# Two transformer-like blocks on one core: FFN up products with a wide operand, two FFN steps on GpSimd, first loads in halves

## The chip, the cores and the metric

The kernel runs on one core of a Trainium2 chip. The time is the device time of one execution in microseconds (us); the profile is one execution recorded by the hardware profiler. The engines are named TensorE (PE in the rows; PEld is its weight load), VectorE (DVE), ScalarE (ACT), GpSimd (POOL) and SyncE (SP, which issues most of the DMAs).

## The reference

Two residual blocks follow each other on an input x of 256 positions by 1024 features, all in float32. The first has a state-space branch and an LRU branch, whose results are gated and merged, and then a gated FFN; the second has four branches (delta rule, spatial gating, window attention, memory attention). The part that the change rewrites is the FFN of the first block:

```python
h = rmsnorm(x, ffn_pre_norm[l])
up = causal_dwconv(h @ w_ffn_up[l], ffn_conv_w[l], ffn_conv_b[l])   # 1024 -> 6144, 3 taps
f_gate, f_val = jnp.split(up, 2, axis=-1)
f = (jax.nn.gelu(f_gate, approximate=True) * f_val) @ w_ffn_down[l]  # 3072 -> 1024
x = x + rmsnorm(f, ffn_post_norm[l])
```

## The kernel before

Every large product runs in a split form: an operand is cut into a high part (rounded by a copy to the 32-bit matmul format) and a low part (operand less high part), and hi x hi, hi x lo and lo x hi are added up in PSUM. The activation's two parts lie side by side in one tile HX, so that `hx[:, k]` is the high part's 256 positions followed by the low part's 256.

The weights come as one long list of chunks, each of two halves of 128 x 1024 (512 KB). The class `Weights` loads the halves in order on SyncE's queue (`load`, line 87) into three raw buffers, makes the high half on ScalarE (line 112) and the low half on VectorE (line 113), and holds five halves of each. `next` is called once a chunk and has the halves split up to five ahead of the chunk's first. `split_pieces` does the same for the first two halves in four pieces each, so that the first product can start early.

There are three ways to run a chunk. `proj_fm` (lines 434 to 455) takes 48 matmuls of 256 columns: `mm3` three times over eight k and two groups of 128 output features; its result lies in PSUM. With `kouter` it goes over k outside. `proj_wide` (lines 457 to 473) takes 32 matmuls: for every k and group, the low weights with the high part (256 columns), and the high weights with both parts at once (512 columns); the second half of the bank is then copied to SBUF by ScalarE (line 471) and added to the first by VectorE (line 472), so its result lies in SBUF. `proj_tm` is the form with positions on the partitions.

The FFN up projection is 12 pairs of chunks (lines 1075 to 1090): the gate chunk (a = 0) and the value chunk (a = 1) of 256 features each. Each goes through `proj_fm`, then a convolution of three taps (`conv`: the last tap with the bias on ScalarE, line 607, the other two on VectorE, line 610). Then come a GELU on ScalarE (line 1086), the product of the two on VectorE (line 1087), and the split of the product into FH (ScalarE, line 353) and FL (VectorE, line 354), the operands of the down projection. TensorE's instructions run in the order of the program; those of the other engines are put in order by a planner, except in the first part of the program, where ScalarE's and VectorE's are in the order written. PSUM has four banks for these products (`pp`), and temporaries come from two rotating sets (`t` with five buffers, `pt` with four).

At the start (lines 276 to 295) SyncE issues the transposed activations XT in two transfers of 512 KB, each followed by a weight half, then one more half, then x; the columns of parameters that the first scaling needs come over ScalarE's queue.

Of the kernel before, what the change touches and what calls it, by code (L numbers as in the profile page):

```python
# [8 lines left out]
F32 = mybir.dt.float32  # L9
F32R = mybir.dt.float32r  # L10
AF = mybir.ActivationFunctionType
ALU = mybir.AluOpType
# [6 lines left out]
HW = 1024  # L19
# [47 lines left out]
class Weights:  # L67
# [14 lines left out]
    def load(self, n):  # L82
        n = min(n, len(self.halves))
        while self.nd < n:
            j = self.nd
            raw = self.pool.tile([P, HW], F32, tag="wraw", name=f"wraw{j}", bufs=self.raw_bufs)
            self.loaded = self.nc.sync.dma_start(raw, self.halves[j])
            self.raw[j] = raw
            self.nd += 1

# [106 lines left out]
def two_blocks_kernel(  # L197
# [27 lines left out]
    nc = tc.nc  # L225
# [12 lines left out]
    def pbank(name):  # L238
        return pp.tile([P, 512], F32, tag="pp", name=name)

    def act8(tag, name, dt=F32, n=NT):
        return big.tile([P, n, S], dt, tag=tag, name=name)

    def hilo(name):

        t = big.tile([P, NT, 2, S], F32R, tag="HX", name=name)
        return t[:, :, 0, :], t[:, :, 1, :], t

    def tmp(name, n=512, tag="t", bufs=NTP):
        return tp.tile([P, n], F32, tag=tag, bufs=bufs, name=name)  # L250

    def v2(ap):
        return ap.rearrange("p (j t) -> p j t", j=2)
# [19 lines left out]
    W = Weights(tc, wp, chunks, 3, 5)  # L273
# [3 lines left out]
    pc = cp.tile([P, NCOL], F32, name="pc")  # L277
    nc.scalar.dma_start(pc[:, 0:8], pcol[:, 0:8])
    XT = act8("b2", "XT")
    for g in range(2):  # L280
        nc.sync.dma_start(XT[:, 4 * g : 4 * g + 4, :],
                          xT[g].rearrange("p (k t) -> p k t", k=4))
        W.load(g + 1)
    W.load(3)
    wsmall = cp.tile([P, 8, 24], F32, name="wsmall")
    pr = cp.tile([P, NROW], F32, name="pr")
# [65 lines left out]
    def split(hi, lo, src):  # L352
        i = nc.scalar.copy(hi, src)
        nc.vector.tensor_tensor(out=lo, in0=src, in1=hi.bitcast(F32), op=ALU.subtract)
        return i
# [72 lines left out]
    def mm3(o, wh, wl, xh, xl, first, last):  # L428

        nc.tensor.matmul(o, wh, xh, start=first, stop=False)  # L430
        nc.tensor.matmul(o, wh, xl, start=False, stop=False)  # L431
        nc.tensor.matmul(o, wl, xh, start=False, stop=last)  # L432

    def proj_fm(name, xh, xl, kouter=False):

        wh, wl = W.next()
        if kouter:
            ps = [pbank(f"{name}_{j}")[:, 0:S] for j in range(2)]
            for k in range(8):
                for j in range(2):  # L440
                    f = slice(j * P, (j + 1) * P)
                    mm3(ps[j], wh[k][:, f], wl[k][:, f], xh[:, k, :], xl[:, k, :],
                        k == 0, k == 7)
                if k % 2 == 1 and k < 7:
                    yield
            return ps, None
        b = pbank(name)
        ps = [b[:, 0:S], b[:, S : 2 * S]]
        for j in range(2):
            f = slice(j * P, (j + 1) * P)  # L450
            for k in range(8):
                mm3(ps[j], wh[k][:, f], wl[k][:, f], xh[:, k, :], xl[:, k, :], k == 0, k == 7)
                if k % 4 == 3 and j + k < 8:
                    yield
        return ps, v2(b)

    def proj_wide(name, hx, o=None):

        wh, wl = W.next()
        ps = [pbank(f"{name}_{j}") for j in range(2)]  # L460
        o = v2(tmp(f"{name}_s")) if o is None else o
        for j in range(2):
            f = slice(j * P, (j + 1) * P)
            for k in range(8):
                a = (ps[j][:, 0:S], wl[k][:, f], hx[:, k, 0, :])
                b = (ps[j], wh[k][:, f], hx[:, k].rearrange("p a t -> p (a t)"))
                for i, p in enumerate((b, a) if k == 0 else (a, b)):
                    nc.tensor.matmul(*p, start=k + i == 0, stop=k == 7 and i == 1)  # L468
                if k % 4 == 3 and j + k < 8:
                    yield  # L470
            nc.scalar.copy(o[:, j, :], ps[j][:, S : 2 * S])
            nc.vector.tensor_tensor(out=o[:, j, :], in0=ps[j][:, 0:S], in1=o[:, j, :], op=ALU.add)
        return [o[:, j, :] for j in range(2)]
# [126 lines left out]
    def conv(outs, ps, wname, tiles, n, taps, bname=None):  # L600

        for o, p, i in zip(outs, ps, tiles):
            w = col(wname, (taps - 1) * n + i)
            if bname is None:
                nc.scalar.activation(o, p, AF.Identity, scale=w)
            else:
                nc.scalar.activation(o, p, AF.Identity, scale=w, bias=col(bname, i))
        for o, p, i in zip(outs, ps, tiles):
            for d in range(1, taps):
                nc.vector.scalar_tensor_tensor(  # L610
                    o[:, d:S], in0=p[:, 0 : S - d], scalar=col(wname, (taps - 1 - d) * n + i),
                    in1=o[:, d:S], op0=ALU.mult, op1=ALU.add)


    HH, HL, HX = hilo("HX1")
# [353 lines left out]
    def block1(HH, HL, HX):  # L969

        late = []
        for p in range(4):
            ps, b = yield from proj_fm(f"ly{p}", HU, LU, p == 0)
            late.append((p, ps, b))
            while late and "rms" in wv.events:
                i, ps, b = late.pop(0)
                o = GY[:, 2 * i : 2 * i + 2, :]
                if b is not None:
                    nc.vector.tensor_tensor(
                        out=o, in0=b, in1=rbc.unsqueeze(1).to_broadcast([P, 2, S]), op=ALU.mult)  # L980
# [7 lines left out]
        for p in (4, 5, 0, 1, 2, 3):  # L988
            ps, _ = yield from proj_fm(f"xbc{p}", HH, HL)
# [15 lines left out]
        for p in range(4):  # L1005
            ps = yield from proj_wide(f"lx{p}", HX)
# [12 lines left out]
        for i in range(4):  # L1019
            n, c = divmod(i, 2)  # L1020
            q = slice(512 * c, 512 * c + 512)
# [15 lines left out]
        for c in range(2):  # L1037
            q = slice(512 * c, 512 * c + 512)
# [3 lines left out]
                    out=MG[:, tt, q], in0=ps, in1=G[0][:, tt, q], op=ALU.mult))  # L1042
# [4 lines left out]
        for c in range(2):  # L1047
            q = slice(512 * c, 512 * c + 512)
# [11 lines left out]
        HH, HL, HX = hilo("HX2")  # L1060
# [6 lines left out]
        for p in range(2):  # L1067
            _, b = yield from proj_fm(f"mk{p}", em["h"], em["l"])
# [4 lines left out]
        FH = [act8(f"b{(3, 6, 7)[i]}", f"FH{i}", F32R) for i in range(3)]  # L1073
        FL = [act8(f"b{(9, 1, 8)[i]}", f"FL{i}", F32R) for i in range(3)]
        for p in range(12):
            cv = []
            for a in range(2):
                ps, _ = yield from proj_fm(f"fu{a}_{p}", HH, HL, p + a == 0)
                c = v2(tmp(f"fc{a}_{p}"))
                i = 24 * a + 2 * p  # L1080
                conv([c[:, 0, :], c[:, 1, :]], ps, "ffn_conv_w", (i, i + 1), 48, 3,
                     "ffn_conv_b")
                cv.append(c)
                if a == 0:
                    yield
            nc.scalar.activation(cv[0], cv[0], AF.Gelu_apprx_tanh)
            nc.vector.tensor_tensor(out=cv[0], in0=cv[0], in1=cv[1], op=ALU.mult)
            q = slice(2 * (p % 4), 2 * (p % 4) + 2)
            last = split(FH[p // 4][:, q, :], FL[p // 4][:, q, :], cv[0])
            yield  # L1090

        O = []
        HH, HL, HX = hilo("HX3")
# [635 lines left out]
    def program():  # L1729
        with tc.manual_schedule(engines={nc.scalar.engine, nc.vector.engine}):  # L1730
            constants()
            for g in range(2):
                for k, _ in enumerate(W.split_pieces(4)):
                    feature(4 * g + k, XT, HU, LU)
                more_loads(g)
            W.split(4)
            for tt in range(2):
                nc.scalar.activation(NRM[:, 0:1024], X[:, tt, :], AF.Square,
                                     accum_out=rx[:, tt : tt + 1])
            nc.scalar.activation(rx, rx, AF.Sqrt, bias=eps1, scale=1.0 / D)  # L1740
            nc.vector.reciprocal(rx, rx)
            dtab.append(small_w(0, 16, "wdt"))
            baab.append(small_w(16, 8, "wba"))
            nc.scalar.activation(ea, row("ssm_a_log"), AF.Exp)
            nc.scalar.activation(ea2, row("a_log_2"), AF.Exp)
            nc.vector.tensor_scalar(nlam, pc[:, lamc : lamc + 8], -1.0, None, op0=ALU.mult)
        yield from block1(HH, HL, HX)
# [139 lines left out]
```

## Time and profile before

| | us |
|---|---|
| median of 3 runs (lowest to highest) | 826.16 (826.12 to 826.82) |
| the profiled execution | 825.72 |
| its span, first to last instruction | 824.0 |
| TensorE busy | 809.6 (98%) |
| VectorE busy | 612.2 (74%) |
| ScalarE busy | 524.6 (64%) |
| GpSimd busy | 61.0 (7%) |

Busy shares are means over stages that differ. A matmul's recorded duration overlaps with the next one's, so its price is the distance from one start to the next. A wait is put down to the release that came last. Transfers are shown by their issue; when they landed shows in who waited for them.

### The profile page before, as it was taken

The numbers are of one execution on the slowest core, as the hardware profiler recorded it, in microseconds if no ns is written. First come the engines' busy times: TensorE is split into PE (matmuls) and PEld (weight loads), VectorE is DVE, ScalarE is ACT, GpSimd is POOL, SyncE is SP. The second block draws the span as 40 slices with busy tenths as digits, with TensorE's granted clock in tenths as the row PEclk, the third lists the DMA queues.
The fourth block names the chain that finished last, engine by engine and source line by source line (L and its number), as shares of the span: only waits on it lengthen the run. The fifth ranks groups of instructions, "written<-read, shape, count | busy, mean of one in ns | idle before, by whom it ended". The sixth has DMA issues, their size and how long they took to land.

```text
span 824.0 us, 13302 instructions
## 1 busy us (share of the span) xinstructions
PE 809.6 (98%) x5060; PEld 721.0 (87%) x5060; DVE 612.2 (74%) x1026; ACT 524.6 (64%) x820; POOL 61.0 (7%) x101
## 2 busy tenths in 40 slices
PE   6999999999999999999999999999999999999997
PEld 6999888888889999999988889888888888888886
DVE  5989789889689788888744697877786647566583
ACT  7575988895656666565643478956976555544452
POOL 0000000000110000000000100028830000000000
PEclk9999999999999999999999999999999999999999
DMA  8545435556754655555555544542454344555551
GB/s 310 204 172 212 153 104 207 177 205 201 257 186 149 216 189 185 182 177 191 201 196 193 192 158 151 182 157 104 169 156 149 130 143 167 202 190 192 190 193 52
DMA packets 41248, 147.12 MB, mean 179 GB/s; under 512 B 4896, under 2 KB 5152, under 8 KB 41056
## 3 DMA queue, kind: packets, MB, share of 16 engines
q1 hardware_dynamic: 40464, 145.35, 51.1%
q0 software_dynamic: 576, 0.92, 0.5%
q8 instruction: 40, 0.66, 0.3%
q14 instruction: 24, 0.20, 0.1%
q10 hardware_dynamic: 144, 0.00, 0.0%
HBM read 144.94 MB, written 1.31 MB: 177 GB/s over the span
## 4 chain that ended last, share of the span: by engine, by line
PE 92%; DVE 5%; ACT 1%; DMA 1%; issue 1%; DVEq 0%; SPq 0%; ACTq 0%
PE z L468 8%; PE fu L432 6%; PE fu L431 6%; PE fu L430 6%; PE g L430 5%; PE g L432 5%; PE g L431 5%; PE lx L468 3%; PE fd L431 3%; PE fd L432 3%; PE fd L430 3%; PE up L430 2%; PE up L431 2%; PE up L432 2%; PE o L432 2%; PE o L430 2%
## 5 line engine op out<-in xcount | busy, mean ns | idle before, releaser
L113 DVE TENSOR_TENSOR wlo<-wraw,whi 128x1024 fp32r<-128x1024 f32 x256 | 311.9, 1226 | 131.6 <-ACT whi L112 130.1
L112 ACT CAST whi<-wraw 128x1024 fp32r<-128x1024 f32 x256 | 266.3, 1049 | 198.4 <-PE fu L431 48.0
L430 PE MATMUL fu<-HX,whi 128*128 128x256 f32 x384 | 108.7, 283 | 0.0
L431 PE MATMUL fu<-HX,whi 128*128 128x256 f32 x384 | 108.7, 283 | 0.0
L432 PE MATMUL fu<-HX,wlo 128*128 128x256 f32 x384 | 108.7, 283 | 0.0
L430 PE MATMUL g<-whi,HX 128*128 128x512 f32 x192 | 76.7, 399 | 0.0
L432 PE MATMUL g<-whi,HX 128*128 128x512 f32 x192 | 74.9, 390 | 0.0
L431 PE MATMUL g<-wlo,HX 128*128 128x512 f32 x192 | 74.8, 390 | 0.0
L430 PEld LDWEIGHTS fu<-HX,whi 128*128 128x128 f32 x384 | 73.7, 192 | 0.0
L431 PEld LDWEIGHTS fu<-HX,whi 128*128 128x128 f32 x384 | 73.7, 192 | 0.0
L432 PEld LDWEIGHTS fu<-HX,wlo 128*128 128x128 f32 x384 | 73.7, 192 | 0.0
L468 PE MATMUL z<-HX,whi 128*128 128x512 f32 x192 | 70.1, 402 | 0.0
L468 PE MATMUL z<-HX,wlo 128*128 128x256 f32 x192 | 51.0, 286 | 0.0
L610 DVE SCALAR_TENSOR_TENSOR fc<-fu,pc,fc 128x255 f32<-128x255 f32 (+1 forms) x96 | 43.8, 478 | 1.6
L432 PEld LDWEIGHTS g<-whi,HX 128*128 128x128 f32 x192 | 36.0, 188 | 7.7
L431 PEld LDWEIGHTS g<-wlo,HX 128*128 128x128 f32 x192 | 36.1, 188 | 7.2
L430 PEld LDWEIGHTS g<-whi,HX 128*128 128x128 f32 x192 | 36.1, 188 | 7.2
L431 PE MATMUL fd<-wlo,FH 128*128 128x512 f32 (+1 forms) x120 | 41.7, 347 | 0.0
L430 PE MATMUL fd<-whi,FH 128*128 128x512 f32 (+1 forms) x120 | 41.6, 347 | 0.0
L432 PE MATMUL fd<-whi,FL 128*128 128x512 f32 (+1 forms) x120 | 41.6, 347 | 0.0
L468 PEld LDWEIGHTS z<-HX,whi 128*128 128x128 f32 x192 | 35.5, 188 | 6.8 <-issue 0.9
L468 PEld LDWEIGHTS z<-HX,wlo 128*128 128x128 f32 x192 | 36.2, 189 | 1.5
(539 smaller groups left out, 1922.7 us busy)
## 6 DMA issues: line engine op xcount, KB each, us to landing
wraw<-in_w_in_dram SPq DMA_DIRECT2D x130, 512.0 KB, 3.8
wraw<-in_w_fu_dram SPq DMA_DIRECT2D x48, 512.0 KB, 3.8
wraw<-in_w_fd_dram SPq DMA_DIRECT2D x24, 512.0 KB, 3.7
wraw<-in_w_o_dram SPq DMA_DIRECT2D x16, 512.0 KB, 3.5
wraw<-in_w_up_dram SPq DMA_DIRECT2D x16, 512.0 KB, 3.4
wraw<-in_w_pa_dram SPq DMA_DIRECT2D x8, 512.0 KB, 3.6
wraw<-in_w_pb_dram SPq DMA_DIRECT2D x8, 512.0 KB, 4.4
wraw<-in_w_mk_dram SPq DMA_DIRECT2D x4, 512.0 KB, 4.1
```

What stands on the lines that cost most here:

```text
L112: nc.scalar.copy(hi, raw)
L113: nc.vector.tensor_tensor(out=lo, in0=raw, in1=hi.bitcast(F32), op=ALU.subtract)
L430: nc.tensor.matmul(o, wh, xh, start=first, stop=False)
L431: nc.tensor.matmul(o, wh, xl, start=False, stop=False)
L432: nc.tensor.matmul(o, wl, xh, start=False, stop=last)
L468: nc.tensor.matmul(*p, start=k + i == 0, stop=k == 7 and i == 1)
L610: nc.vector.scalar_tensor_tensor(o[:, d:S], in0=p[:, 0 : S - d], scalar=col(wname, (taps - 1 - d) * n + i), in1=o[:, d:S], op0=ALU.mult, o ...
```

## The change

Three things change. The first transfers: XT now comes in pieces of two, two and four k-tiles, and the first weight half in two halves, interleaved as XT piece, weight piece, XT piece, weight piece, XT piece (`between` is called behind each weight piece); then the second and third half come as before. The FFN up projection: all chunks but the first go through `proj_wide`, with the sum in a temporary of the `pt` set. The FFN's product and the low part of it run on GpSimd for the first eleven pairs, on VectorE for the last; the copy to FH stays on ScalarE.

```diff
--- before.py
+++ after.py
@@ -84,7 +84,12 @@
         while self.nd < n:
             j = self.nd
             raw = self.pool.tile([P, HW], F32, tag="wraw", name=f"wraw{j}", bufs=self.raw_bufs)
-            self.loaded = self.nc.sync.dma_start(raw, self.halves[j])
+            if j == 0:
+                for q in (slice(0, HW // 2), slice(HW // 2, HW)):
+                    self.nc.sync.dma_start(raw[:, q], self.halves[j][:, q])
+                    self.between()
+            else:
+                self.loaded = self.nc.sync.dma_start(raw, self.halves[j])
             self.raw[j] = raw
             self.nd += 1
 
@@ -277,10 +282,15 @@
     pc = cp.tile([P, NCOL], F32, name="pc")
     nc.scalar.dma_start(pc[:, 0:8], pcol[:, 0:8])
     XT = act8("b2", "XT")
-    for g in range(2):
-        nc.sync.dma_start(XT[:, 4 * g : 4 * g + 4, :],
-                          xT[g].rearrange("p (k t) -> p k t", k=4))
-        W.load(g + 1)
+    pieces = [(0, 2), (2, 4), (4, 8)]
+
+    def x_piece():
+        a, b = pieces.pop(0)
+        v = xT[a // 4].rearrange("p (k t) -> p k t", k=4)
+        nc.sync.dma_start(XT[:, a:b, :], v[:, a % 4 : a % 4 + b - a, :])
+
+    x_piece()
+    W.between = x_piece
     W.load(3)
     wsmall = cp.tile([P, 8, 24], F32, name="wsmall")
     pr = cp.tile([P, NROW], F32, name="pr")
@@ -1075,7 +1085,11 @@
         for p in range(12):
             cv = []
             for a in range(2):
-                ps, _ = yield from proj_fm(f"fu{a}_{p}", HH, HL, p + a == 0)
+                if p + a == 0:
+                    ps, _ = yield from proj_fm(f"fu{a}_{p}", HH, HL, True)
+                else:
+                    ps = yield from proj_wide(f"fu{a}_{p}", HX,
+                                              v2(tmp(f"fs{a}_{p}", tag="pt", bufs=4)))
                 c = v2(tmp(f"fc{a}_{p}"))
                 i = 24 * a + 2 * p
                 conv([c[:, 0, :], c[:, 1, :]], ps, "ffn_conv_w", (i, i + 1), 48, 3,
@@ -1084,9 +1098,12 @@
                 if a == 0:
                     yield
             nc.scalar.activation(cv[0], cv[0], AF.Gelu_apprx_tanh)
-            nc.vector.tensor_tensor(out=cv[0], in0=cv[0], in1=cv[1], op=ALU.mult)
+            eng = nc.gpsimd if p < 11 else nc.vector
+            eng.tensor_tensor(out=cv[0], in0=cv[0], in1=cv[1], op=ALU.mult)
             q = slice(2 * (p % 4), 2 * (p % 4) + 2)
-            last = split(FH[p // 4][:, q, :], FL[p // 4][:, q, :], cv[0])
+            fh, fl = FH[p // 4][:, q, :], FL[p // 4][:, q, :]
+            last = nc.scalar.copy(fh, cv[0])
+            eng.tensor_tensor(out=fl, in0=cv[0], in1=fh.bitcast(F32), op=ALU.subtract)
             yield
 
         O = []
```

## Rows read from the trace of the kernel before

**Rows 1.** The page's chain that ended last: share of the span by engine.
```profile
PE 92%; DVE 5%; ACT 1%; DMA 1%; issue 1%; DVEq 0%; SPq 0%; ACTq 0%
```

**Rows 2.** Table by stage: stretch, length, busy us by engine, clock, DMA share, GB/s.
```profile
265.00:405.00 140.00, 140.00 (x1164) 139.78 (x1163) 115.17 (x168) 85.53 (x123) 0.00 (x0) 1.00 0.57 193
...
288.51:380.67 92.16, 92.16 (x771) 92.16 (x769) 76.87 (x113) 55.02 (x81) 0.00 (x0) 1.00 0.55 186
```

**Rows 3.** The FFN up tile's third product: ns min/median/max, first and last start.
```profile
L432 PE MATMUL fu<-HX,wlo x384: 283/283/283, 265.7 to 403.6; 128*128 128x256 f32 x192
```

**Rows 4.** Chain that ended last in order of time: start us, us, what.
```profile
609.65 5.57 PE z L468 x32
```

**Rows 5.** Groups by shape, LRU projection: busy us, mean ns | idle before.
```profile
L471 ACT COPY lx_s<-lx 128x256 f32<-128x256 f32 x7 | 2.6, 378 | 2.1 <-PE lx L468 2.1
L472 DVE TENSOR_TENSOR lx_s<-lx,lx_s 128x256 f32<-128x256 f32 x6 | 2.5, 420 | 0.8 <-ACT lx_s L471 0.8
...
L610 DVE SCALAR_TENSOR_TENSOR XC<-lx_s,pc,XC 128x254 f32<-128x254 f32 x5 | 2.3, 479 | 0.0
```

**Rows 6.** Timeline of VectorE, LRU and FFN up projections: start us, us, instruction.
```profile
112.37 1.66 DVE L610 SCALAR_TENSOR_TENSOR XC<-lx_s,pc,XC 128x254 f32<-128x254 f32 x4
...
340.07 1.23 DVE L113 TENSOR_TENSOR wlo<-wraw,whi 128x1024 fp32r<-128x1024 f32 x1 [0.52 <-ACT whi L112]
```

**Rows 7.** Groups by shape, 270 to 400 us (FFN up projection).
```profile
L610 DVE SCALAR_TENSOR_TENSOR fc<-fu,pc,fc 128x254 f32<-128x254 f32 x44 | 21.1, 481 | 1.4
...
L1087 DVE TENSOR_TENSOR fc<-fc,fc 128x512 f32<-128x512 f32 x11 | 7.6, 692 | 0.4
L354 DVE TENSOR_TENSOR FL<-fc,FH 128x512 fp32r<-128x512 f32 x11 | 7.5, 685 | 0.0
```

**Rows 8.** The memory input's tile, GpSimd: ns min/median/max, first and last start.
```profile
L913 POOL TENSOR_TENSOR MT<-MT,MEM x4: 1465/1769/2330, 222.6 to 228.4; 128x512 f32<-128x512 f32 x4
```

**Rows 9.** Timeline of GpSimd, its third and fourth multiplication.
```profile
226.91 1.48 POOL L913 TENSOR_TENSOR MT<-MT,MEM 128x512 f32<-128x512 f32 x1
...
228.35 1.47 POOL L913 TENSOR_TENSOR MT<-MT,MEM 128x512 f32<-128x512 f32 x1
```

**Rows 10.** Timeline of VectorE beside them and just behind.
```profile
227.15 0.68 DVE L1052 TENSOR_TENSOR G<-pb,G 128x512 f32<-128x512 f32 x1
227.75 0.92 DVE L916 SCALAR_TENSOR_TENSOR EL<-MT,pc,EH 128x256 fp32r<-128x256 f32 x1
228.59 1.77 DVE L1053 TENSOR_TENSOR MG<-MG,G 128x512 f32<-128x512 f32 x1
...
232.08 0.47 DVE L916 SCALAR_TENSOR_TENSOR EL<-MT,pc,EH 128x256 fp32r<-128x256 f32 x1
232.47 0.68 DVE L1053 TENSOR_TENSOR MG<-MG,G 128x512 f32<-128x512 f32 x1
```

**Rows 11.** Timeline of ScalarE at the start, with idle time before and its releaser.
```profile
6.16 0.40 ACT L127 CAST whi<-wraw 128x256 fp32r<-128x256 f32 x1 [3.43 <-DMA wraw<-in_w_in_dram]
```

**Rows 12.** Timeline of TensorE at the start.
```profile
7.03 0.58 PE L430 MATMUL ly<-HU,whi 128*128 128x256 f32 x1 [7.03 <-ACT HU L627]
```

**Rows 13.** DMA view of 0 to 12 us: GB/s in 40 equal slices.
```profile
GB/s 0 0 0 0 0 0 218 164 220 220 344 372 399 425 396 410 423 423 423 410 410 423 423 423 410 410 437 410 423 437 410 423 410 423 423 423 423 410 410 437
```

**Rows 14.** Timeline of SyncE's DMA queue: issues.
```profile
3.41 0.96 SPq L291 DMA_DIRECT2D X<-in_x_dram  x2
9.32 0.33 SPq L87 DMA_DIRECT2D wraw<-in_w_in_dram  x1
```

**Rows 15.** Timeline of ScalarE, 13 to 22 us.
```profile
13.70 1.05 ACT L112 CAST whi<-wraw 128x1024 fp32r<-128x1024 f32 x1 [0.85 <-DMA wraw<-in_w_in_dram]
...
19.17 2.93 ACT L112 CAST whi<-wraw 128x1024 fp32r<-128x1024 f32 x3
```

**Rows 16.** Timeline of VectorE, the same stretch.
```profile
20.23 1.23 DVE L113 TENSOR_TENSOR wlo<-wraw,whi 128x1024 fp32r<-128x1024 f32 x1 [2.20 <-ACT whi L112]
```

**Rows 17.** Timeline of TensorE, the same stretch.
```profile
21.63 0.28 PE L432 MATMUL ly<-HU,wlo 128*128 128x256 f32 x1
```

## The prediction

> **What bounds the kernel now.** First the chain of work that ended last: 92% of it is TensorE [rows 1], so only an edit that shortens TensorE's own work, or that makes TensorE wait or stops it from waiting, can move the end. Next the table by stage, for the stretch that the change rewrites: in the FFN up projection TensorE is busy in all of the 140 us, GpSimd does nothing, VectorE is busy 115 us and ScalarE 86 us [rows 2]. Sixteen whole chunks lie in the second row of that table: 92.16 us, so 5.76 us a chunk and 11.52 us a pair (gate chunk and value chunk), of which VectorE works 76.87/8 = 9.61 us. The group of the third product says the same from TensorE's side: 384 matmuls, started from 265.7 to 403.6, are 383 steps of 0.360 us, three matmuls each, so 0.120 us a matmul and 48 x 0.120 = 5.76 us a chunk [rows 3]. TensorE has no gap there; VectorE has 11.52 - 9.61 = 1.91 us of room a pair.
>
> **The FFN up products.** A chunk is 48 products of 256 columns now. Twenty-three of the 24 chunks (all but the first, which keeps its order over k) become 16 products of 256 columns and 16 of 512: as many columns, 16 instructions fewer. The price of that form is in this trace, since the second block uses it: a whole chunk of 32 such matmuls with nothing between took 5.57 us [rows 4]; I take 5.58. Gain: 23 x (5.76 - 5.58) = 4.1 us, on the path for as long as TensorE has no gap. Bounds: 4.4 us with 5.57, and nothing if the products have to wait.
>
> **What VectorE gets and loses.** Each wide chunk adds two copies on ScalarE and two adds on VectorE (hi part from PSUM, lo part from SBUF); in the LRU projection they take 0.378 and 0.420 us [rows 5], so the adds are 4 x 0.42 = 1.68 us a pair by duration and about 4 x 0.35 = 1.4 us by what one delays the next (neighbours overlap by some 0.07 us: four convolution steps show 1.66 us of busy time against 4 x 0.48 [rows 5, 6]). The two 512-wide steps that go to GpSimd take 0.692 and 0.685 us [rows 7], about 1.25 us with the same overlap. The convolution now reads the sum in SBUF, not PSUM: 0.479 us in the LRU projection against 0.481 here, no change [rows 5, 7]. So VectorE's own work is 9.61 - 1.25 + 1.4 = 9.8 us a pair (9.3 if its eight convolution steps also take 1.66 us per four, not 4 x 0.48), and TensorE's new pair is 11.16 us. ScalarE has 55.02/8 = 6.9 us a pair [rows 2] and gets 4 x 0.378: 8.4 us, so it is not the bound.
>
> **What GpSimd takes from VectorE.** The stage itself has no GpSimd row. The nearest are the four 128x512 multiplications of the memory input, 1.47 to 2.33 us each, median 1.77 [rows 8]. While the third and fourth ran [rows 9], VectorE's instructions with two SBUF operands were held up: one of 0.47 us took 0.92, and the residual add took 1.77 where its next instance took 0.68, so it was held for 1.09 us; the product with one operand in PSUM kept its 0.68 us in the middle of the third [rows 10]. So the two engines exclude each other for part of the GpSimd span. I read it as 1.1 us of each; the rest of the 1.47 to 2.33 us is GpSimd's own start and waiting. This matters more after the change than before it: now six VectorE instructions a pair read two SBUF operands (four low parts of weights and the two 512-wide steps), afterwards twelve (four low parts, eight convolution steps), and only the four adds from PSUM can run beside GpSimd. Eleven pairs put two steps on GpSimd (the twelfth keeps VectorE): 2 x 1.1 = 2.2 us, less about 0.3 us in which an add from PSUM lies beside it. VectorE's demand is then 9.8 + 2.2 - 0.3 = 11.7 us a pair (bounds: 10.8 with the quick convolution and 0.7 of overlap, 12.0 with none), against TensorE's 11.16.
>
> That builds up 11 x 0.54 = 5.9 us of lag over the stage. It costs nothing until TensorE meets it. Chunk n starts at 265.46 + 5.76 n [rows 3]; the low half made from 340.07 to 341.30 [rows 6] belongs to the second half of the chunk after next (n = 14, from 346.10) and is needed there after 1.44 us, at 347.54, so 6.2 us of lag are covered by the five buffers. PSUM covers about as much: four banks, two a chunk, so a chunk's adds may end up to 5.58 us after its last product. Behind the stage comes the down projection, which needs the last product only in its last chunk. So the lag is nearly all covered; I charge 0.3 us of stalls (bounds: 0 with the demand of 10.8; (12.0 - 11.16) x 11 - 6.2 = 3.0 us with 12.0). The waits that are added (ScalarE's copy of the product behind GpSimd's multiplication, GpSimd's subtraction behind that copy) hold back the next weight casts and taps on ScalarE's queue, which has 2.8 us of room a pair; that is inside the same cover.
>
> The Trainium skill speaks against this part. "SBUF — State Buffer", section "Who interferes with whom", says that a VectorE instruction with two SBUF inputs and a GpSimd instruction that reads SBUF contend, and that the later one is blocked until the other's end. The held and unheld rows agree on which instructions are blocked; for how long they show 1.09 us, less than any GpSimd span. By whole spans the time would be that of the first rival below.
>
> **The first loads.** ScalarE's first cast waits until 6.16 us for the first 512 KB of weights, behind 512 KB of activations, and TensorE starts at 7.03 [rows 11, 12]. With the first four transfers 256 KB each, the first pair of pieces is 512 KB, not 1 MB; at the 420 GB/s that this stretch comes to [rows 13] that is 1.2 us sooner, so TensorE's first product at about 5.85. The total is unchanged, and this gives the gain back: the fourth weight half, issued at 9.32, is queued behind the two loads of x issued from 3.41 [rows 14], and its cast starts at 13.70 after a wait for that transfer. From there ScalarE runs ten more instructions with no gap over 0.03 us to the cast at 19.17 [rows 15]; the low half of that cast is made from 20.23 to 21.46 [rows 16], and TensorE's third chunk uses it at 21.63 [rows 17]. So whatever TensorE gains at its start is cut there to 21.63 - 21.46 = 0.17 us. The two more issues on SyncE's queue come ahead of x and of weights that the transfers before them hold back anyway. I take 0.1 us of gain; bounds 1.2 (if the fourth half came sooner too) and -0.3 (smaller rows a little slower, or the issues in the way).
>
> **Sum.** 4.1 - 0.3 + 0.1 = 3.9 us. The profiled execution took 825.72 us (span 824.0), so it would take 821.8 us; the median of the three runs is 0.44 us above it, 826.16, and gives 822.3 us.
>
> **The rivals.** First, slower: VectorE and GpSimd become the bound of the FFN up stage. Place: pairs 0 to 10. With h the time that one GpSimd step holds VectorE, the demand is 9.5 + 2h us a pair (9.8 less 0.3 of overlap), and the stall is 11 x (9.5 + 2h - 11.16) - 6.2 us. It eats the whole gain of 4.2 us at h = 1.30; at the shortest recorded span, 1.47, it is 7.9 us and the kernel takes 829.9; at the median span, 1.77, it would be 14.5 us, 836.5. For it: the spans, and twice as many VectorE instructions that can be held. Against it: the one full hold in the trace is 1.09 us. Whole spans are what the page of the skill named above would give.
> Second, no change: the cover is smaller than I think, because casts, copies and taps wait in a fixed order on ScalarE and VectorE, and PSUM has two chunks of room where it had four. With 3 us less of it the stall is about 3 us and the time 825; or the wide chunks don't keep their pace beside this load and save nothing, in which case it is 826. For it: my middle demand is above TensorE's pace. Against it: ScalarE's room, and the second block's wide chunks at 5.57.
> Third, more: the start keeps its whole 1.2 us because the early loads come in another order; then 821.2. Against it: the transfer-bound cast at 13.70.
>
> **How the numbers follow.** Forecast 53%, about 821.4 to 823.5; first rival 13%, second 20%, third 14%. Measurement of this kernel can tell about 0.2%, 1.65 us, from no change. Faster by more than that (below 824.5): forecast and third rival, 0.67. Within it: the second, 0.20. Slower (above 827.8): the first, 0.13. The range goes down to 820.6, the third rival with the better ends of the products, and up to 827.0, the second with the lower part of the first; the rest of the first is left out.
>
> **What would show it.** Wide chunks at 5.58 us and TensorE without a gap from 271 to 400 us: the products are right. VectorE's busy share in the stage near 90% or above, and low halves and convolution steps stretched by about 1.1 us beside a GpSimd step: the hold is right. Gaps of TensorE late in the stage, released by low halves or by the adds: the first or second rival. TensorE's first product near 5.9 us, but its third chunk still near 21.3: the start is right. The forecast is wrong if low halves are needed much earlier than the buffers suggest, or if the order that the planner gives ScalarE and VectorE elsewhere shifts by microseconds.

## The result, and the profile after

The changed kernel takes 840.37 us (median of 4 runs, 839.9 to 841.19) where the kernel before took 826.14 beside it: a ratio of 1.0172, 95% interval 1.0154 to 1.0190. It is 14.2 us slower; 822.3 us and "faster" were forecast. The profiled execution has a span of 838.1 us against 824.0, so the two traces show the whole difference.

The share of the chain that ended last, by engine, from the page of the changed kernel, against [rows 1]:

```profile
PE 70%; DVE 13%; ACT 7%; DMA 4%; issue 3%; POOL 3%; SPq 0%; DVEq 0%; ACTq 0%; POOLq 0%
```

TensorE carried 92% of the end and now carries 70%. The starts of its groups say where. Its first product came 1.44 us earlier (5.59 us, against 7.03 in [rows 12]), the SSM stage at 62 us began 3.6 us later, and this stays until the FFN up projection (first product at 269.03, against 265.47). That stage is 8.9 us longer (147.11 us from its first product to the first of the down projection, 138.24 before), the down projection 1.7 us more, and behind it the distance stays at 14.1. So there are two losses: about 3.6 us at the start and about 10.6 in and right behind the FFN up stage.

The start. These are ScalarE, VectorE and TensorE of the changed kernel in the timeline (start us, us, instruction, idle time before and its releaser), to be read beside [rows 11], [rows 12] and [rows 15 to 17]:

```profile
4.73 0.40 ACT L132 CAST whi<-wraw 128x256 fp32r<-128x256 f32 x1 [1.99 <-DMA wraw<-in_w_in_dram]
...
14.87 1.05 ACT L117 CAST whi<-wraw 128x1024 fp32r<-128x1024 f32 x1 [1.12 <-DMA wraw<-in_w_in_dram]
...
21.40 2.36 DVE L118 TENSOR_TENSOR wlo<-wraw,whi 128x1024 fp32r<-128x1024 f32 x2 [2.20 <-ACT whi L117]
...
5.59 0.58 PE L440 MATMUL ly<-HU,whi 128*128 128x256 f32 x1 [5.59 <-ACT HU L637]
...
22.68 0.39 PE L442 MATMUL ly<-HU,wlo 128*128 128x256 f32 x1 [0.45 <-DVE wlo L118]
```

The first cast comes 1.43 us sooner, but the fourth weight half lands later: its cast starts at 14.87, not 13.70. The chain behind it moves by the same 1.17 us, and the third chunk's first product with a low half starts at 22.68, not 21.63. That is two executions; in eleven other traces with the old loads the cast starts at 13.35 to 13.93, in the three with the new ones at 14.29 to 14.87. The half is issued earlier than before (8.70 us, against 9.32 in [rows 14]), so it is the transfers that are late. The DMA view of the changed kernel for 0 to 12 us (GB/s in 40 equal slices) shows it, beside [rows 13]:

```profile
GB/s 0 0 0 0 0 0 61 234 311 374 405 273 212 300 266 287 253 280 369 355 403 314 396 382 423 410 410 423 410 396 410 437 437 423 410 437 410 410 382 410
```

In both kernels the first bytes move in the seventh slice (1.8 to 2.1 us); the first cast is earlier because it waits for 512 KB, not 1 MB. But from 3.3 to 5.4 us the stream runs at 212 to 300 GB/s, where the kernel before is at 372 to 425, and by 12 us it has moved 3.63 MB, not 3.97.

The FFN up stage. From the table by stage of the changed kernel (columns as in [rows 2]), the part in which GpSimd's products come 12.9 us apart:

```profile
291.60:404.80 113.20, 104.11 (x587) 89.14 (x586) 85.73 (x140) 71.64 (x123) 29.93 (x18) 1.00 0.51 164
```

The wide chunks do run at 5.59 us, one after another up to the tenth. Then every second one takes 7.3 us and a pair 12.92. No engine is full in this row: TensorE works 92% of it (its first wait comes at 334 us), VectorE 76%, ScalarE 63%, GpSimd 26%. So the stage is not bound by an engine's load. The waits of the stage in the changed kernel (engine line waited for: us in total, times, longest us) name the links:

```profile
ACT FH L1105 <- POOL fc L1102: 25.7, 10, 2.7
ACT fc L617 <- DVE fs L482: 20.4, 20, 1.8
DVE fs L482 <- ACT fs L481: 18.9, 9, 2.1
PEld fu L478 <- DVE wlo L118: 13.1, 8, 2.0
```

ScalarE stands before GpSimd's product (2.6 us a pair), VectorE before ScalarE's bank copy that is queued behind it, and TensorE before low halves that are queued behind VectorE's adds. Followed back, this closes. One turn of it in the chain that ended last of the changed kernel (start us, us, what):

```profile
349.06 0.49 DVE fc L620
...
349.68 2.15 POOL fc L1102
...
351.85 0.62 ACT FH L1105
352.47 0.27 ACT fs L481
352.74 0.51 ACT fc L617
...
353.34 0.80 DVE fc L620
...
354.56 1.22 DVE wlo L118
...
356.18 0.34 DVE fs L482
...
356.55 0.41 ACT fc L617
...
357.05 0.62 ACT fc L1100
357.67 0.95 ACT whi L117
...
358.64 0.30 DVE wlo L118
358.94 0.85 issue
359.78 0.42 DVE fs L482
360.20 1.14 DVE wlo L118
...
361.98 0.49 DVE fc L620
...
362.60 2.15 POOL fc L1102
```

From one product of GpSimd (L1102) to the next are 12.92 us: 2.15 on GpSimd, 3.4 on ScalarE (hi copy L1105, bank copy, two taps, gelu L1100, weight cast), and the rest on VectorE. Some 4.5 us of the turn split weights (a cast and three low halves, the second of them with the 0.85 us behind it), which need nothing of the product. They are in the loop only because they stand in order between its links on ScalarE and VectorE.

### The profile page after: what moved, and what is told of

Read it like the earlier page. It is cut to its first block, busy times and chain, and to the rows that moved or that the text cites. A ratio compares the mean times of both kernels' runs of the same rounds, so it can differ in the third digit from the quotient of the medians.

```text
span 838.1 us, 12677 instructions
## 1 busy us (share of the span) xinstructions
PE 809.3 (97%) x4692; PEld 700.5 (84%) x4692; DVE 618.7 (74%) x1050; ACT 539.6 (64%) x866; POOL 98.7 (12%) x123
## 4 chain that ended last, share of the span: by engine, by line
PE 70%; DVE 13%; ACT 7%; DMA 4%; issue 3%; POOL 3%; SPq 0%; DVEq 0%; ACTq 0%; POOLq 0%
PE z L478 8%; DVE wlo L118 5%; PE g L440 5%; PE g L442 5%; PE g L441 5%; DVE fc L620 3%; PE lx L478 3%; POOL fc L1102 3%; DMA wraw<-in_w_in_dram 2%; PE fd L441 2%; PE fd L442 2%; PE fd L440 2%; ACT whi L117 2%; PE up L440 2%; PE up L441 2%
## 5 line engine op out<-in xcount | busy, mean ns | idle before, releaser
L478 PE MATMUL fu<-HX,whi 128*128 128x512 f32 x368 | 126.0, 396 | 0.0
L478 PE MATMUL fu<-HX,wlo 128*128 128x256 f32 x368 | 96.1, 281 | 10.5 <-DVE wlo L118 10.4
L478 PEld LDWEIGHTS fu<-HX,wlo 128*128 128x128 f32 x368 | 69.4, 189 | 17.1 <-DVE wlo L118 13.1
L478 PEld LDWEIGHTS fu<-HX,whi 128*128 128x128 f32 x368 | 65.9, 188 | 12.0
L620 DVE SCALAR_TENSOR_TENSOR fc<-fs,pc,fc 128x255 f32<-128x255 f32 x92 | 47.9, 520 | 7.2 <-ACT fc L617 4.9
L617 ACT ACTIVATE fc<-fs,pc 128x256 f32<-128x256 f32 x46 | 27.6, 601 | 22.5 <-DVE fs L482 22.5
L1102 POOL TENSOR_TENSOR fc<-fc,fc 128x512 f32<-128x512 f32 x11 | 22.6, 2057 | 140.1 <-DVE fc L620 140.1
```

Of the source, the lines that this page charges most:

```text
L620: nc.vector.scalar_tensor_tensor(o[:, d:S], in0=p[:, 0 : S - d], scalar=col(wname, (taps - 1 - d) * n + i), in1=o[:, d:S], op0=ALU.mult, o ...
L1102: eng.tensor_tensor(out=cv[0], in0=cv[0], in1=cv[1], op=ALU.mult)
```

## The experiments

Theory A: the loop of waits through the engines' fixed orders makes the stage long. Theory B: GpSimd's reads hold VectorE up. For the start: late transfers, or another order. Ratios are to the kernel before in the same runs.

**First loads alone.** The first two hunks of the diff.

> Only the first loads of the change (256 KB pieces); FFN as before. In the changed kernel TensorE is 1.15 us late from its third chunk on and 3.62 us late from 62 us on, before the FFN begins. If the first loads alone cause both, this takes 826.1 + 3.6 = 829.8 us, with TensorE starting near 5.6 us. Rival: only the slower transfers (1.15 us) belong to the loads and the other 2.5 us come from the planner seeing another FFN; then 827.3. My prediction's own step (a gain of 0.1) would give 826.0.

831.02 us, ratio 1.0056 (1.0041 to 1.0071): 4.5 us slower. With the FFN part alone (below, +9.8) the medians add up to 14.3, the whole loss; but this run is not quite the changed kernel's start, whose loss by its trace is 3.6 us. What differs is a fall of TensorE's clock, shown with the last run of the start.

**Wide products alone.** Only the hunk of `proj_wide`; the product and its lo part stay on VectorE.

> Only the wide FFN up products; the FFN's product and low part stay on VectorE, first loads as before. Theory A (ScalarE's copy to FH waits in order behind GpSimd's multiplication and holds up the bank copies): no GpSimd here, so TensorE keeps 5.59 us a chunk and the kernel takes 826.1 - 4 = 822.2 us. Theory B (GpSimd takes VectorE's time): the same, 822.2. Theory C (the wide form's own chain from copy to add to tap on two engines in order is too long beside the weight splits): slower than 826, with chunks at 6 us or more late in the stage.

821.95 us, ratio 0.9949 (0.9932 to 0.9966). Every wide chunk takes 5.59 us and the stage 134.4. Its table for eight pairs:

```profile
299.20:388.70 89.50, 89.50 (x514) 77.96 (x514) 84.71 (x144) 66.37 (x114) 0.00 (x0) 1.00 0.54 189
```

TensorE has no gap and VectorE works 10.59 of 11.19 us a pair. This version is faster than both kernels.

**GpSimd's part alone.** Only the last hunk, with the old products.

> Only the FFN's product and low part on GpSimd; products of 256 columns as before, first loads as before. Theory A: ScalarE waits about 2 us a pair for GpSimd, but has 4.6 us of room a pair and no bank copies behind it, so TensorE is not reached: 826.1. Theory B: VectorE's convolution reads PSUM and is not held, its demand is 9.6 - 1.25 + 2.2 = 10.6 us against 11.5: 826.1 too. If it is slower than 828, GpSimd's part is harmful without the wide form.

826.82 us, ratio 1.0006 (0.9996 to 1.0015): no effect. The chunks stay at 5.76 us. The convolution still reads PSUM, and VectorE, relieved of two steps, has more room.

**The FFN part whole**, with the old first loads.

> The FFN part of the change whole (wide products and GpSimd), first loads as before. If start and FFN add up, the loss here is what the changed kernel loses from the FFN on, 14.2 - 3.6 = 10.6 us: 836.8 us. If it is 832 or less, the late start made the FFN worse.

836.33 us, ratio 1.0116 (1.0101 to 1.0132): pairs of 12.92 us and the changed kernel's waits. Two edits, one worth -4.6 us by the medians and one worth nothing, make +9.8 together.

**The hi copy on GpSimd too**, so that ScalarE waits for nothing there.

```
-            last = nc.scalar.copy(fh, cv[0])
+            last = nc.gpsimd.tensor_copy(fh, cv[0]) if p < 11 else nc.scalar.copy(fh, cv[0])
```

> Wide products and GpSimd as in the change, first loads as before, but the copy to FH moves from ScalarE to GpSimd too (pairs 0 to 10). GpSimd then does three steps a pair and nothing on ScalarE waits for it. Theory A (ScalarE's copy to FH waits in order behind GpSimd and holds up the next bank copy): the wait is gone, 822 to 823 us, chunks at 5.59. Theory B (GpSimd holds VectorE): a third step adds up to 1.1 us of hold a pair, so worse than the run with two steps (836.3): 840 or more.

837.1 us, ratio 1.0131 (1.0116 to 1.0146): no better, so theory A alone fell here. ScalarE's wait is gone, but a third operation reads beside VectorE, whose low halves take 1.50 us on average instead of 1.22, and the pair is 12.9 again.

**Two idle products of GpSimd a pair**, for which nobody waits, beside the wide products.

```
+            if p < 11:
+                for _ in range(2):
+                    nc.gpsimd.tensor_tensor(out=idle, in0=cv[1], in1=cv[1], op=ALU.mult)
```

> Wide products with the FFN's product and low part on VectorE as in the wide run (821.95 us), and besides two 128x512 multiplications a pair on GpSimd whose result is not used and for which no instruction of the pair waits: the hold on VectorE by itself. Theory A: little or nothing, 822 to 823. Theory B: VectorE has 11.2 us a pair and needs 9.8 + 1.25 + 2.2 = 13.2, so about 1.5 to 2 us a pair lost once the buffers are used up: 830 or more.

827.88 us, ratio 1.0018 (1.0009 to 1.0027), 5.9 us above the wide products alone. Five pairs in the table by stage:

```profile
342.41:402.62 60.21, 57.23 (x322) 48.73 (x320) 59.69 (x90) 40.90 (x71) 12.79 (x10) 1.00 0.51 175
```

And a GpSimd pair with VectorE beside it in the timelines of the same run:

```profile
354.59 2.63 POOL L1094 TENSOR_TENSOR idle<-fc 128x512 f32<-128x512 f32 x2 [9.40 <-DVE fc L610]
...
355.06 2.44 DVE L610 SCALAR_TENSOR_TENSOR fc<-fs,pc,fc 128x255 f32<-128x255 f32 x2
```

VectorE is busy 99% of 12.04 us a pair: here it is full, as the first rival had it. Two convolution steps take 1.22 us on average instead of 0.48, so VectorE loses some 0.74 us to each GpSimd operation of 1.3. That is what was left of the operation when the step came: the first step starts 0.47 us after the first operation, and the second step ends at 357.50, 0.28 us after GpSimd's end at 357.22, with 0.48 us of its own work. So it was held until about 0.2 us before that end. The Trainium skill, "SBUF — State Buffer", section "Who interferes with whom", has the later instruction blocked until the other's end, and the trace agrees but for these 0.2 us.

**The hi copy later**: still on ScalarE, but behind the next pair's gate taps.

```
+                    with tc.issue_after(tap.ins):
+                        nc.scalar.copy(fh, f)
```

> Wide products and GpSimd as in the change, first loads as before, but the copy to FH of a pair stays on ScalarE and is put behind the convolution taps of the next pair's gate chunk, when GpSimd has long finished (GpSimd's subtraction follows it). Theory A: 822 to 823 us, chunks at 5.59. Theory B: the holds are all there, so 836 as with the copy in its old place.

831.16 us, ratio 1.0059 (1.0044 to 1.0074): 5.2 us of the 9.8 come back from one instruction's place. The work is the same (GpSimd's lo part moves with the copy), so place matters; but 9.2 us over the wide products are left.

**One GpSimd operation a pair**: the product on VectorE, the lo part on GpSimd.

```
-            eng.tensor_tensor(out=cv[0], in0=cv[0], in1=cv[1], op=ALU.mult)
+            nc.vector.tensor_tensor(out=cv[0], in0=cv[0], in1=cv[1], op=ALU.mult)
```

> Wide products, first loads as before; VectorE keeps the FFN product, the hi copy follows it as before, and only the lo part's subtraction runs on GpSimd. Nobody waits for it before the down projection. Output unchanged. One GpSimd operation a pair that reads two activations, and no added wait on ScalarE. The hold theory: VectorE gives up 0.68 us a pair (the lo part) and is held about 0.75 us once, so its 10.59 us of 11.19 a pair hardly move and the time stays at 821.5 to 823.5. If any work of GpSimd in this stage delays the loop, as two idle products did (827.9), the time is 825 to 828.

822.84 us, ratio 0.9958 (0.9941 to 0.9975). An operation that nobody waits for, and that takes 0.68 us off VectorE for a hold of about as much, is neither gain nor loss within 1 us.

**The wait alone**: GpSimd reads no activations; it clears an unused row, and ScalarE's hi copy waits for that.

```
+                nc.gpsimd.memset(idle, 0.0)
+                nc.gpsimd.memset(idle[:, 0:768], 0.0)
+                copies.append(nc.scalar.activation(fh, cv[0], AF.Identity, bias=zc))
```

> Wide products, first loads as before. VectorE keeps the FFN product and its lo part, so GpSimd reads no activations. GpSimd only clears an unused row twice after each product (a clear of 128x1024 took 0.95 us in the kernel before, so some 1.7 us together), and ScalarE's hi copy waits for that, in the place that it has in the changed kernel: directly ahead of the second bank copy of the next gate chunk. The lo part is held back behind the next gate convolution. Output unchanged. If the wait in ScalarE's order is what costs the most (the loop through ScalarE, VectorE, GpSimd), pairs take about 12.4 to 12.9 us where the wide products alone took 11.19, and the time is 831 to 837, with VectorE's convolution steps at their free 0.48 us. If the loss comes from GpSimd's accesses holding VectorE up, the pairs stay at 11.2 to 11.5 and the time at 822 to 825.

822.22 us, ratio 0.9948 (0.9931 to 0.9964): nothing is lost. In this order the hi copy stood behind the first tap; the next kernel differs from this one by having it ahead of both taps:

> As the run with the wait alone (GpSimd clears an unused row, ScalarE's hi copy waits for that, VectorE keeps the arithmetic), with ScalarE's order set closer to the changed kernel's: the hi copy ahead of both taps and of the second bank copy of the next gate chunk, not behind the first tap. Output unchanged. The first placement took 822.2, as the wide products alone did. If the wait in this place makes the loop of 12.9 us a pair by itself, the time is 831 to 837; if a wait of this length on ScalarE fits into what the stage has in hand, and it takes GpSimd's reads beside VectorE to make the loop, it stays at 821.5 to 823.5, with VectorE's free convolution steps at 0.48 us and its share of the stage above 90%.

821.95 us, ratio 0.9950 (0.9933 to 0.9966). ScalarE's wait over eight pairs in this run:

```profile
ACT FH L1116 <- POOL idle L1115: 5.6, 8, 0.9
```

And its table for the same pairs:

```profile
299.20:388.70 89.50, 89.50 (x513) 77.95 (x512) 83.87 (x144) 66.72 (x112) 13.60 (x16) 1.00 0.57 185
```

ScalarE waits 0.7 us a pair, where it waits 2.6 in the changed kernel, and TensorE has no gap. So a wait for GpSimd on ScalarE's queue need not cost anything. But in both runs VectorE's order differed from the changed kernel's (it had the product and the lo part again), and GpSimd's two clears take 1.7 us, not 2.15, so the last two runs pin both engines' order through the stage to that of the FFN part run whole.

**Waits kept, reads taken away, same order.** GpSimd clears where it multiplied.

```
-            eng.tensor_tensor(out=cv[0], in0=cv[0], in1=cv[1], op=ALU.mult)
+                for _ in range(3):
+                    t = nc.gpsimd.memset(cv[1], 0.0)
+                with tc.issue_after(t.ins):
+                    nc.gpsimd.memset(cv[0], 0.0)
```

> The change's FFN part (wide products, old first loads) with GpSimd's reads taken away and everything else in place: instead of the product GpSimd clears the up half three times and then the gate half (a clear of 128x512 should take about 0.5 us, from 0.95 for 128x1024, so about 2.2 us where the product held the loop for 2.15), instead of the lo part it clears the gate half and the lo buffer. It waits for the same, ScalarE's hi copy waits for it, and ScalarE's and VectorE's order through the stage is pinned to that of the FFN part run whole (836.3), up to the last pair. The product itself is left out, so the output differs. If the loop of in-order waits alone makes the 12.9 us a pair, the time is 833 to 838. If it takes GpSimd's reads beside VectorE, the time is 821.5 to 825.

832.71 us, ratio 1.0073 (1.0057 to 1.0090), 10.8 us above the wide products alone. VectorE's convolution steps in this run, as a group (330 to 400 us: busy us, mean ns | idle before):

```profile
L613 DVE SCALAR_TENSOR_TENSOR fc<-fs,pc,fc 128x255 f32<-128x255 f32 (+1 forms) x42 | 20.2, 481 | 2.8 <-ACT fc L609 1.7
```

And one turn in its chain that ended last:

```profile
345.87 0.54 POOL fc L1096
...
347.56 0.48 POOL fc L1098
348.06 0.62 ACT FH L1103
...
349.56 0.50 DVE fc L613
...
358.49 0.54 POOL fc L1096
```

Nothing is held (481 ns, as in [rows 7]; the same section of the Trainium skill says that a GpSimd instruction which only writes does not contend, and here the trace agrees), and yet the turn is the changed kernel's, in 12.62 us. Its convolution step is 0.50 us where the changed kernel's was 0.80: that is as much as the two turns differ by.

**Reads kept, ScalarE's wait taken away, same order.** The product goes to an unused row, and the hi copy reads the activated gate half.

```
+            prod = v2(idle[:, 0:512]) if p < 11 else cv[0]
+            eng.tensor_tensor(out=prod, in0=cv[0], in1=cv[1], op=ALU.mult)
```

> The counterpart: GpSimd does the change's product and lo part as there, reads and all, but writes the product to an unused row, and ScalarE's hi copy reads the activated gate half, so ScalarE waits for nothing of GpSimd. ScalarE's and VectorE's order through the stage is pinned to that of the FFN part run whole (836.3). The gate and up halves' product is left out of what goes on, so the output differs. If the waits alone make the loop, the time falls to 822 to 824. If GpSimd's reads alone do it, it stays at 833 to 837. If it takes both, this run lies between, as the run with the late hi copy did (831.2).

826.26 us, ratio 0.9995 (0.9985 to 1.0004), 4.3 us above the wide products alone. The same group in this run:

```profile
L613 DVE SCALAR_TENSOR_TENSOR fc<-fs,pc,fc 128x254 f32<-128x254 f32 (+1 forms) x47 | 32.2, 686 | 2.5 <-ACT fc L609 2.0
```

And five pairs of its table by stage:

```profile
342.24:401.61 59.37, 57.46 (x324) 48.92 (x323) 55.04 (x81) 40.34 (x72) 17.78 (x10) 1.00 0.56 177
```

The convolution steps are held (686 ns) and VectorE is busy 11.0 of 11.87 us a pair. So in the changed kernel's order a turn of waits with nothing held on VectorE costs 10.8 us, the reads without ScalarE's wait cost 4.3, and both together 14.4. Theory A's loop is shown, and theory B's hold too, but they are no separate shares. The four clears in the loop were made as long as the changed kernel's product (2.17 us together), and that product is so long because VectorE's low half holds it up in its turn, here in the timelines of the changed kernel:

```profile
349.45 1.22 DVE L118 TENSOR_TENSOR wlo<-wraw,whi 128x1024 fp32r<-128x1024 f32 x1
349.68 2.14 POOL L1102 TENSOR_TENSOR fc<-fc,fc 128x512 f32<-128x512 f32 x1 [8.75 <-DVE fc L620]
```

The product ends 1.15 us after the low half; the first one of the stage, with no low half beside it, takes 1.29 us in all. With these 0.85 us taken off, the turn would be about 11.8 us, and the forecast's own formula would leave 11 x (11.8 - 11.18) - 6.2, less than 1 us of stalls. That is an estimate, and no run has it: how much of the 10.8 us the waits would cost without the reads was not measured.

**The start: smaller rows alone.** The kernel before with its first activations in two transfers whose rows are 2 KB, not 4.

```
+        nc.sync.dma_start(
+            XT.rearrange("p (g k) t -> p g k t", g=2)[:, :, 2 * g : 2 * g + 2, :],
+            xT.rearrange("g p (k t) -> p g k t", k=4)[:, :, 2 * g : 2 * g + 2, :])
```

> The kernel before with as many first transfers, each of 512 KB, but the two of the activations in rows of 2 KB (k-tiles 0, 1, 4, 5 and then 2, 3, 6, 7) instead of 4 KB. If rows of 2 KB make the change's first loads slow, the third weight half lands 0.5 us or more after the 9.89 us of before; if it is the number of transfers (about 1.1 us each whatever their size), it lands at 9.9. In the second case the time stays at 826.5; in the first it is 827 to 828 if ScalarE's and VectorE's order stays as before.

826.54 us, ratio 1.0005 (0.9995 to 1.0014). The fourth half's cast starts at 14.42, 0.72 us late and later than in any other trace with transfers of 512 KB, so smaller rows do slow the stream; what the two added transfers do was not run alone. The planner's order stays that of before, and no time is lost that can be measured.

**The start: the change's loads with the order of before.** Two weight casts are held behind the taps that they followed before.

```
+                with self.tc.issue_after(t.ins):
+                    nc.scalar.copy(hi, raw)
```

> Only the first loads in the change's pieces, with two casts of weight halves (the 15th and the 19th) held behind the convolution taps that they follow in the kernel before, so that ScalarE's and VectorE's order up to the tables is that of before but for one swap. Output unchanged. The change of the first loads alone took 831.0 against 826.5. If its loss is mostly the order that moved (some 2.5 us between 53 and 62 us, and more that follows), this run is at 826.5 to 828.5. If it is the transfers that land 1.16 us late, the order does not matter and it stays at 830 to 831.5.

827.06 us, ratio 1.0008 (0.9998 to 1.0017). With the order held, 3.9 of the 4.5 us are gone (some 0.5 of them because the loads came sooner in this run; its fourth half's cast starts at 14.29). The order can be seen on ScalarE in the timelines, here first of the kernel before, then of the run with the first loads alone:

```profile
41.31 1.02 ACT L607 ACTIVATE bBC<-xbc,pc 128x256 f32<-128x256 f32 x2
42.22 1.04 ACT L112 CAST whi<-wraw 128x1024 fp32r<-128x1024 f32 x1
...
52.76 1.03 ACT L607 ACTIVATE XS<-xbc,pc 128x256 f32<-128x256 f32 x2
53.67 1.05 ACT L112 CAST whi<-wraw 128x1024 fp32r<-128x1024 f32 x1
...
56.30 1.28 ACT L994 ACT_TABLE_LOAD   x1 [0.23 <-DVE bBC L610]
```

```profile
43.73 1.05 ACT L117 CAST whi<-wraw 128x1024 fp32r<-128x1024 f32 x1 [0.90 <-DMA wraw<-in_w_in_dram]
44.69 1.01 ACT L617 ACTIVATE bBC<-xbc,pc 128x256 f32<-128x256 f32 x2
...
53.25 2.93 ACT L117 CAST whi<-wraw 128x1024 fp32r<-128x1024 f32 x3
56.08 1.03 ACT L617 ACTIVATE XS<-xbc,pc 128x256 f32<-128x256 f32 x2
...
59.15 1.04 ACT L117 CAST whi<-wraw 128x1024 fp32r<-128x1024 f32 x1
60.21 1.28 ACT L1004 ACT_TABLE_LOAD   x1
```

First a cast that waits for its transfer stands ahead of taps which it followed before; they start at 44.69, not 41.31. Then a third cast stands ahead of the next taps and another ahead of the table load, and the load comes 3.9 us later, where the first product of these chunks had been only 1.0 us late (34.88 us against 33.85). TensorE waits for what follows the load, 2.96 us in the run with the first loads alone and 2.56 us in the changed kernel, which has the same order. What comes behind that wait differs. These are TensorE's timeline and a row of the table by stage, first of the run with the first loads alone, then of the changed kernel (the clock is the third value from the end):

```profile
62.19 0.70 PE L719 MATMUL pcb<-bBC 128*128 128x256 f32 x2 [2.96 <-ACT bBC L1004]
64.00:66.00 2.00, 2.00 (x10) 1.91 (x9) 2.00 (x6) 0.63 (x1) 0.00 (x0) 0.50 0.82 320
...
61.90 0.70 PE L719 MATMUL pcb<-bBC 128*128 128x256 f32 x2 [2.56 <-ACT bBC L1004]
64.00:66.00 2.00, 2.00 (x18) 1.95 (x17) 2.00 (x5) 0.63 (x1) 0.00 (x0) 1.00 0.70 272
```

In the first the granted clock is at the lower of its two levels (1.2 GHz, not 2.4), and 10 matmuls run where the other has 18. TensorE is 3.9 us late at the end of its wait there and 5.5 at the end of these chunks (76.97 us, against 71.50 in the kernel before); the changed kernel is 3.6 us late at both. So some 1.5 us of the loss of the first loads alone are the lower clock behind a wait that the order made, and the changed kernel did not pay them.

## Why the prediction was wrong, point by point

**The wide products: right.** The forecast was 5.58 us a chunk and 4.1 us of gain; alone they take 5.59 and give 4.2 by the ratio, 4.6 by the medians. VectorE's load was forecast as 9.8 us a pair with two steps on GpSimd; in the changed kernel it is 85.73 us in 113.2, so 9.8 us per 12.92. Without GpSimd's help they leave VectorE 0.6 us of room a pair (10.59 of 11.19).

**The hold: right in kind, misread in size.** It was taken as a fixed 1.1 us from [rows 10], less than GpSimd's span, and set against the section of the Trainium skill that the prediction cites. The rows agree with that section: the residual add starts 0.24 us after GpSimd's fourth multiplication (228.59 against 228.35) and ends at 230.36, which with 0.68 us of its own work means that it was held until 229.68, 0.14 us before the multiplication's end. So a hold lasts as long as what is left of the other operation: 0.74 us on average with the idle products, about 0.3 us for the convolution step in the changed kernel's turn. The demand of 11.7 us of VectorE a pair was too much (11.0 with the reads alone), and the first rival, VectorE as the full engine, is not what happened: VectorE is 76% busy in the slow stretch. That rival had the sign, and the size of the FFN part (829.9 to 836.5, and 836.3 came out), but not the mechanism.

**The failed step: "The waits that are added ... that is inside the same cover".** It charged the waits against ScalarE's room of 2.8 us a pair. Here the wait was not load: it joined what stood before it and behind it, on three engines, into one turn, and the turn had a length of its own whatever the engines' shares were. That length, 12.92 us, takes the place of the forecast's 11.7 in its own formula: 11 x (12.92 - 11.18) = 19.1 us of lag, less the cover of 6.2, gives 12.9 us of stalls, and the stage is 147.11 - 134.4 = 12.7 us longer than with the wide products alone. So the period failed, and in this run the cover came out. (For the run with the clears the formula gives 9.6 us and the stage is 10.1 longer; for the run without ScalarE's wait it gives 1.4, against 3.2.) The charge of 0.3 us and its upper bound of 3.0 came from the load alone. GpSimd's own part of the turn had no term either: its product takes 2.15 us, 0.85 of them held by VectorE's low half, where the forecast counted only what GpSimd takes from VectorE.

**The first loads: the cap was right, its price was not.** TensorE started at 5.59 us, and the gain was cut at the transfer-bound cast, as forecast. But the price of smaller rows and more issues, -0.3 us at most, was 1.17 us of later landing. "Splitting DMAs into smaller chunks may allow some to start sooner", says the Trainium skill, "Perfetto Trace Analysis", section "DMA Optimizations", and the first piece did; the same section prefers larger ones, and the stream's rate bears that out. The larger term was in no sum: with these loads the planner put weight casts ahead of convolution taps at 40 to 60 us. In the changed kernel TensorE is 1.15 us late at 35 us and 3.6 at 62; in the run of the first loads alone the order and the lower clock behind its wait are most of the 3.9 us that came back. The forecast named it only among what would make it wrong, without a price or a chance.

**The rivals' chances.** "Slower" had 13%. The trace of before could not show the turn, but the program could have: hi copy behind GpSimd's product, bank copy behind the hi copy on ScalarE, VectorE's add behind that.

**What stays open.** Why the order with the product on VectorE bears the same kind of wait at no cost: both orders have the links, the clears there come 11.2 to 11.3 us apart, and whether it is the instructions that moved or the shorter clears was not separated. Open too is the turn with GpSimd's product at its free 1.29 us, and the 1.7 us in the down projection. The latter seems to go with GpSimd's reads: from its first product to its last the down projection takes 66.2 us in the kernel before and with the clears, 67.0 in the run without ScalarE's wait, 68.0 in the changed kernel.

## What to carry to other kernels

Before work goes to another engine and an in-order engine waits for its result, write down the closed turn: what stands behind the waiting instruction, who waits for that, and back to the producer, with everything that lies in order between, needed or not. In these runs its length was the period where it exceeded the bound engine's, and no room in an engine's busy share paid for it. And where a planner sets the order, an edit of the first microseconds can move instructions much later; its price is read from a run with the order held.

## What the hardware showed that was not expected

A 128x512 product of two SBUF tiles on GpSimd took 1.29 us alone and 2.10 to 2.15 where a low half was running on VectorE, so it waits itself, too, and ends 1.15 us after the low half. A clear of 128x512 took 0.53 and disturbed nobody. VectorE's convolution steps that came while such a product ran lost what was left of it, less about 0.2 us. And the loads up to the fourth weight half landed 1.2 us later with their first MB in 256 KB pieces of 2 KB rows, though the first cast came earlier.
